# A transformer layer in float32: the first norm's gain and bias applied behind the transposes and later in token layout, with the residual loaded in place

## The chip, the cores and the metric

One core of a Trainium2 chip runs the whole kernel. The metric is the device time of one execution in microseconds (us), the median over several runs.

## The reference

One layer on x of 1024 tokens by 1024 features, all in float32 (S = D = 1024, F = 2816):

```
h    = x @ w_in                                  # attention heads and a gated spatial group
mix  = concat(diff_attention(h), spatial_gate(h)) @ w_out
x    = layer_norm(ALPHA * x + mix, ln1_g, ln1_b) # the first norm
g    = causal_conv3(x @ w_gate)                  # along the tokens
up   = x @ w_up
f    = (silu(g) * up) @ w_down
x    = layer_norm(ALPHA * x + f, ln2_g, ln2_b)   # the second norm
```

where layer_norm(y, g, b) = (y - mean) * rstd * g + b, with mean and rstd of each token.

## The kernel before

Every float32 product runs as three matmuls: each operand is split into a high part (written by ACT in `split`, L216) and a low part (the rest, by DVE, L217), and L221 to L223 add hi·hi, hi·lo and lo·hi into one PSUM tile. Four engines work beside TensorE (PE): VectorE (DVE), ScalarE (ACT), GpSimd (POOL), and SyncE (SP), whose queue issues most DMAs. Each engine runs its instructions in order; a scheduler that builds the program chooses the order and which buffer a new tile takes, and puts a wait on the last user of that buffer.

The work comes in five stages (times in the profiled execution).

- **Projections and attention**, 0 to 365 us.
- **Output projection**, 365 to 434 us: `mix` for each token tile t of 128 tokens. `fill_x` adds ALPHA·x (loaded by `x_load` into a tile of its own, `xn`) to the product and takes the norm's statistics; `lnorm` then computes the norm. It takes the statistics together (DVE `bn_aggr`), adds EPS, raises to the power -1/2 on POOL (L889), then for each half of 512 columns: (x - mean) * g on DVE (L891), times rstd on ACT (L893) or on DVE (L896), plus b on POOL (L894).
- **Gate stage**, 434 to about 866 us: x @ w_gate and x @ w_up in 22 units u (even: gate, odd: up). A unit is a 2 by 2 block product by Strassen's scheme: seven products P1 to P7 instead of eight, each 12 matmuls of 128x512. Their x operands are A11, A12, A22 and the sums S1 to S4 (QA), their weight operands B11, B21, B22 and the differences T1 to T4 (QB). Tokens 0 to 511 give A11 and A12, tokens 512 to 1023 A21 and A22; each needs x with features on the partitions, so `x1_transp(t)` transposes tile t on PE (L930) and ACT copies it from PSUM (`fA`, L938), and `x1_sums` forms S2 on DVE (L948), S4 on POOL (L950); A22 is added straight from PSUM into S1 (DVE L935) and S3 is formed on POOL (L936). Four products of the first two units run before the sums are needed; `fill_in` puts the transposes of the last two token tiles behind the products i = 0 and i = 1 of `seq`, the sums behind i = 2 and 3.
- **Down stage**, about 866 to 1087 us: the same scheme with w_down (operands `yo` and `do`), in the order of DORDER, P4 and P3 last. `d_out` adds a product's PSUM into x; `finish(t)` is the second norm and the store of tile t. Tiles 4 to 7 are finished behind P4, tiles 0 to 3 behind the last matmuls of P3.
- **Tail**, to 1096 us: the last tile's norm and its store.

In the gate stage a weight quarter is loaded into one of 8 raw buffers (`tslot`, tile `wq`), DVE forms the differences in place (L972), and ACT and DVE write the split operand (`wT`, `wB`) into one of 16 buffers (`kslot`), some seven products ahead of its use. P4, P6 and P7 of a unit add up in one PSUM tile, and ACT copies it out after each (L1009 to L1020), so the next of them waits for that copy:

```
        elif name == "P6":
            A.copy(d1[:, LEFT], a)
        elif name == "P7":
            A.copy(d1[:, RIGHT], a)
```

Of the kernel before, what the change touches and what calls it, by code (L numbers as in the profile page):

```python
# [138 lines left out]
def hybrid_layer_kernel(  # L139
# [735 lines left out]
    def load_row(pool, ap_, name):  # L875
        t = pool.tile([P, D], F32, name=name)
        GP.dma_start(t, bc_row(ap_, D))
        return t

    g1 = load_row(op, ln1_g, "g1")  # L880
    b1 = load_row(op, ln1_b, "b1")
    x1T = {}
# [309 lines left out]
    fill_in = [  # L1192
        lambda: x1_transp(6), lambda: x1_transp(7), lambda: (x1_sums("S1"), prepare(1)),
        lambda: (x1_sums("S2"), prepare(4), x1_sums("S3"), prepare(5), x1_sums("S4")),
    ]
# [65 lines left out]
    for n, name in enumerate(DORDER):  # L1261
# [79 lines left out]
```

## Time and profile before

| | |
|---|---|
| median of 3 runs | 1097.71 us (1096.16 to 1100.11) |
| the profiled execution | 1097.62 us, span 1095.8 us |
| PE, DVE, ACT, POOL busy | 1060.0, 785.4, 485.0, 189.3 us |
| mean granted clock of PE | 0.988 of full speed |

The span is what the trace covers; the rest of an execution's time, 1.8 us, lies around it. A wait is the idle time of an engine ahead of an instruction, put down to the event that released it.

### The profile page before, as it was taken

What the parts mean: (1) busy time and instruction counts of PE and PEld (TensorE: products, weight loads), DVE (VectorE), ACT (ScalarE), POOL (GpSimd) and SP (SyncE); (2) the same over time, 40 slices, a digit from 0 to 9 for tenths busy, and PEclk for the clock granted to TensorE, in tenths of its full rate; (3) what the DMA queues carried; (4) which work ended last, traced back from release to release, by engine and by line L of the source; (5) the groups of instructions that cost most, each with busy time, mean ns of one, the idle gap of its engine ahead of it and who ended that gap; (6) DMA issues with size and microseconds to landing.
All of it is one profiled execution on the core that took longest, in us unless ns stands there. A gap on an engine that the chain in (4) does not pass through costs nothing.

```text
span 1095.8 us, 14041 instructions
## 1 busy us (share of the span) xinstructions
PE 1060.0 (97%) x4974; PEld 874.2 (80%) x4974; DVE 785.4 (72%) x1308; ACT 485.0 (44%) x901; POOL 189.3 (17%) x213
## 2 busy tenths in 40 slices
PE   8999999987999999899999999999999999999996
PEld 6888888876787888678888888888888878888874
DVE  5327246669999648997687677768777589954786
ACT  5511113456777335555344434434544254444441
POOL 2014132228643036400000000000000000000045
PEclk9999999999999999899999999999999999999997
DMA  8400214442200511033332232233235983432322
GB/s 260 150 10 10 96 57 126 107 116 59 58 11 20 181 50 49 11 115 113 118 124 69 106 125 86 104 110 126 67 109 175 315 287 94 135 106 87 106 86 96
DMA packets 57574, 115.92 MB, mean 106 GB/s; under 512 B 7392, under 2 KB 7920, under 8 KB 57504
## 3 DMA queue, kind: packets, MB, share of 16 engines
q1 hardware_dynamic: 56464, 111.70, 31.1%
q0 software_dynamic: 1040, 3.32, 1.1%
q8 instruction: 39, 0.64, 0.2%
q14 instruction: 31, 0.25, 0.1%
HBM read 82.23 MB, written 24.38 MB: 97 GB/s over the span
## 4 chain that ended last, share of the span: by engine, by line
PE 84%; DVE 8%; issue 3%; POOL 3%; DMA 1%; SPq 1%; ACT 0%; DVEq 0%; POOLq 0%; ACTq 0%
PE ps L222 26%; PE ps L221 26%; PE ps L223 26%; PE ps L622 2%; PE ps L608 1%; PE ps L545 1%; PE ps L546 1%; DVE x L891 1%; POOL kl L475 1%; PE ps L357 1%; DVE p L591 1%; DVE mx L558 1%; DMA dq<-w_down 1%; DVE wT L217 0%; PE ps L930 0%
## 5 line engine op out<-in xcount | busy, mean ns | idle before, releaser
L222 PE MATMUL ps<-do,yo 128*128 128x512 f32 x308 | 122.2, 397 | 2.7 <-DVE do L217 2.7
L221 PE MATMUL ps<-do,yo 128*128 128x512 f32 x308 | 120.7, 393 | 2.3 <-ACT do L216 2.3
L223 PE MATMUL ps<-do,yo 128*128 128x512 f32 x308 | 121.6, 395 | 0.0
L217 DVE TENSOR_TENSOR wT<-wq,wT 128x512 fp32r<-128x512 f32 x88 | 63.1, 719 | 34.2 <-ACT wT L216 34.1
L1268 POOL DMA_DIRECT2D g<-ln_g x1 | 0.6, 578 | 477.3 <-DVE do L217 477.3
L216 ACT ACTIVATE wT<-wq 128x512 fp32r<-128x512 f32 x88 | 55.3, 632 | 50.6 <-PE ps L223 43.5
L217 DVE TENSOR_TENSOR yo<-ya,yo 128x512 fp32r<-128x512 f32 x77 | 55.0, 715 | 23.9 <-ACT yo L216 23.8
L222 PEld LDWEIGHTS ps<-do,yo 128*128 128x128 f32 x308 | 58.9, 191 | 16.6 <-DVE do L217 4.2
L221 PEld LDWEIGHTS ps<-do,yo 128*128 128x128 f32 x308 | 58.5, 190 | 14.8 <-ACT do L216 2.8
L216 ACT ACTIVATE yo<-ya 128x512 fp32r<-128x512 f32 x77 | 48.3, 627 | 48.1 <-PE ps L223 46.9
L223 PEld LDWEIGHTS ps<-do,yo 128*128 128x128 f32 x308 | 59.1, 192 | 12.4
L217 DVE TENSOR_TENSOR wB<-wq,wB 128x512 fp32r<-128x512 f32 x66 | 45.8, 697 | 26.8 <-ACT wB L216 20.4
L217 DVE TENSOR_TENSOR do<-dq,do 128x512 fp32r<-128x512 f32 x66 | 47.4, 718 | 23.3 <-ACT do L216 23.3
L216 ACT ACTIVATE wB<-wq 128x512 fp32r<-128x512 f32 x66 | 41.1, 630 | 48.4 <-PE ps L223 33.5
L972 DVE TENSOR_TENSOR wq<-wq,wq 128x512 f32<-128x512 f32 x88 | 60.7, 690 | 2.6
L216 ACT ACTIVATE do<-dq 128x512 fp32r<-128x512 f32 x66 | 41.2, 624 | 48.1 <-DVE yo L217 17.3
L1038 DVE SCALAR_TENSOR_TENSOR c<-g,cw,c 128x1023 f32<-128x1023 f32 (+1 forms) x44 | 56.3, 1279 | 6.5 <-ACT c L1036 6.4
L570 ACT ACTIVATE p<-ps,mx 128x512 f32<-128x512 f32 (+7 forms) x64 | 47.1, 742 | 9.0 <-DVE mx L558 5.9
L221 PE MATMUL ps<-xh,qw 128*128 128x512 f32 x128 | 49.9, 390 | 0.0
L222 PE MATMUL ps<-xl,qw 128*128 128x512 f32 x128 | 49.8, 389 | 0.0
L223 PE MATMUL ps<-xh,qw 128*128 128x512 f32 x128 | 49.8, 389 | 0.0
L221 PE MATMUL ps<-zw,xh 128*128 128x512 f32 x128 | 49.8, 389 | 0.0
(244 smaller groups left out, 2935.8 us busy)
## 6 DMA issues: line engine op xcount, KB each, us to landing
ya<-yd SPq DMA_DIRECT2D x77, 256.0 KB, 2.9
wq<-w_gate SPq DMA_DIRECT2D x44, 256.0 KB, 2.8
wq<-w_up SPq DMA_DIRECT2D x44, 256.0 KB, 2.8
yd<-u SPq DMA_DIRECT2D x22, 512.0 KB, 3.1
dq<-w_down SPq DMA_DIRECT2D x44, 256.0 KB, 4.6
zraw<-w_vz SPq DMA_DIRECT2D x23, 256.0 KB, 3.0
yd<-c SPq DMA_DIRECT2D x11, 512.0 KB, 2.6
qraw<-w_qk SPq DMA_DIRECT2D x8, 512.0 KB, 4.2
```

Of the source, the lines that this page charges most:

```text
L216: A.activation(hi, src, AF.Copy)
L217: (lo_eng or V).tensor_tensor(lo, src, hi.bitcast(F32), op=ALU.subtract)
L221: PE.matmul(po, lhsT=lh, rhs=rh, start=start, stop=False, skip_group_check=onto)
L222: PE.matmul(po, lhsT=lh, rhs=rl, start=False, stop=False, skip_group_check=onto)
L223: PE.matmul(po, lhsT=ll, rhs=rh, start=False, stop=stop, skip_group_check=onto)
L357: PE.matmul(pt[:, c, :], lhsT=vg[t // 2][:, t % 2, g * P : (g + 1) * P], rhs=wsr[:, g, :], start=True, stop=True)
L475: eng.tensor_tensor(o, r[rows], hi, op=ALU.subtract)
L545: PE.matmul(o[:, 0:ww], lhsT=qs[:, qc], rhs=kh[:, kc], start=True, stop=False)
L570: A.activation(p[:, 0:L].rearrange("p (b n) -> p b n", b=nb), sc, AF.Exp, bias=st_mx[n][:, j : j + 1], accum_out=sm[:, j : j + 1],)
L622: PE.matmul(st_o[h, i][:, j * DV : (j + 1) * DV], lhsT=st_at[h, i][kt // 4][:, kt % 4, j], rhs=vr[kt // 2][:, kt % 2, h * DV : (h + 1) * D ...
L972: sub = lambda o, a, b: V.tensor_tensor(q[o], q[a], q[b], op=ALU.subtract)
L1038: V.scalar_tensor_tensor(t[:, n:S], g[:, 0 : S - n], cw[:, f, 2 - n : 3 - n], t[:, n:S], op0=ALU.mult, op1=ALU.add)
```

## The change

The first norm's gain and bias are no longer applied where the norm is computed. `standard(t)` writes (x - mean) * rstd alone: DVE takes the statistics together and forms two small terms, POOL computes rstd and -mean * rstd, and one ACT instruction scales and shifts the whole tile. The gain and bias are applied in two other places:

- behind the transposes, where a feature is a partition: ACT's eviction of each transposed block takes them as a scale and a bias per partition (`gb1`). Transposes come in pairs of token tiles; the last pair stands behind product i = 2. A22 is now written to SBUF too, so the splits and sums read SBUF, and S3 and S4 are formed on DVE.
- in token layout, for the residual of the second norm: `gain(t, c)` on POOL, a multiplication and an addition per half tile, in the gate stage, with g and b of one half broadcast into a `kslot` buffer `gb`.

The right half of x for the residual is loaded straight into x1; the weight quarters of units 0 and 1 are all loaded at t = 3; `finish(4)` to `finish(7)` move from behind P4 to P3's m = 1 to 4, and weights of the last two products are prepared up to 3 steps earlier.

```diff
+    def standard(t):
+        mv = op.tile([P, 32], F32, tag="mv", name=nm("mv"), bufs=3)[:, 0:3]
+        rs = op.tile([P, 32], F32, tag="rs", name=nm("rs"), bufs=3)[:, 0:2]
+        V.bn_aggr(mv[:, 0:2], stats[t])
+        V.tensor_scalar(rs[:, 0:1], mv[:, 1:2], EPS, None, op0=ALU.add)
+        V.tensor_scalar(mv[:, 2:3], mv[:, 0:1], -1.0, None, op0=ALU.mult)
+        GP.tensor_tensor(rs[:, 0:1], rs[:, 0:1], mhalf[:, 0:1], op=ALU.pow)
+        GP.tensor_tensor(rs[:, 1:2], rs[:, 0:1], mv[:, 2:3], op=ALU.mult)
+        A.activation(x1[t], x1[t], AF.Identity, scale=rs[:, 0:1], bias=rs[:, 1:2])
...
         for eg, name in enumerate(names):
-            pt = ps1().rearrange("p (e q) -> p e q", e=4)
-            for e in range(4):
-                PE.transpose(pt[:, e, :], x1[t][:, (eg * 4 + e) * P : (eg * 4 + e + 1) * P], ident)
             for n in range(2):
-                src = pt[:, 2 * n : 2 * n + 2, :]
-                if name == "A22":
-                    f = xf["A21"][n][:, :, tk]
-                    V.tensor_tensor(xf["S1"][n][:, :, tk], f, src, op=ALU.add)
-                    GP.tensor_tensor(f, xf["A11"][n][:, :, tk], f, op=ALU.subtract)
-                else:
-                    A.copy(xf[name][n][:, :, tk], src)
+                pt = ps1().rearrange("p (e q) -> p e q", e=2)
+                f = xf["S1" if name == "A22" else name][n][:, :, tk]
+                for e in range(2):
+                    k = eg * 4 + n * 2 + e
+                    for i in range(2):
+                        PE.transpose(pt[:, e, i * P : (i + 1) * P], x1[t + i][:, k * P : (k + 1) * P], ident)
+                    A.activation(f[:, e], pt[:, e], AF.Identity, scale=gb1[:, 0, k : k + 1], bias=gb1[:, 1, k : k + 1])
                 if name != "A21":
                     hi, lo = xo[name][n]
-                    split(hi[:, :, tk], lo[:, :, tk], src)
+                    split(hi[:, :, tk], lo[:, :, tk], f)
+                if name == "A22":
+                    V.tensor_tensor(f, xf["A21"][n][:, :, tk], f, op=ALU.add)
...
-            if name == "S2":
-                V.tensor_tensor(xf[o][n], xf["S1"][n], xf["A11"][n], op=ALU.subtract)
-            elif name == "S4":
-                GP.tensor_tensor(xf[o][n], xf["A12"][n], xf["S1"][n], op=ALU.subtract)
+            if a:
+                V.tensor_tensor(xf[o][n], xf[a][n], xf[b][n], op=ALU.subtract)
...
     for t in range(NT):
-        x_load(t, 1)
+        nc.sync.dma_start(x1[t][:, RIGHT], x[t * P : (t + 1) * P, RIGHT])
+    for t in range(NT):
...
         fill_x(t, pt, 1)
-        lnorm(op, x1[t], stats[t], x1[t], g1, b1, None, t < NT - 1)
-        if 2 <= t < 6:
-            x1_transp(t - 2)
+        standard(t)
+        if t in (3, 5):
+            x1_transp(t - 3)
+        if t == 3:
+            for u in range(2):
+                w_load(u, ("B11", "B21"))
+            for u in range(2):
+                w_load(u, ("B12", "B22"))
...
+    def gain(t, c):
+        h = RIGHT if c else LEFT
+        if t == 0:
+            gb[c] = kslot([P, 2, 512], "gb", F32)
+            GP.dma_start(gb[c][:, 0], bc_row(ln1_g[h], 512))
+            GP.dma_start(gb[c][:, 1], bc_row(ln1_b[h], 512))
+        r = x1[t][:, h]
+        GP.tensor_tensor(r, r, gb[c][:, 0], op=ALU.mult)
+        GP.tensor_tensor(r, r, gb[c][:, 1], op=ALU.add)
+
+    gains = {(u + 3, "P4"): (u % NT, u // NT) for u in range(2 * NT)}
...
         elif name == "P4":
             start(hi[:, LEFT])
             norm_stats(4 + j, 0)
-            finish(4 + j)
...
-            d_prepare(n * NM + m + DAHEAD)
+            d_prepare(n * NM + m + DAHEAD + (max(0, min(3, m - 3)) if name == "P4" else 3 if name == "P3" else 0))
+            if name == "P3" and m:
+                finish(3 + m)
```

How this changes the order of the instructions is shown at three places. The number after an underscore tells tiles of one name apart.

**POOL at the start of the gate stage.** Before: the S3 differences (L936), the two S4 differences (L950) and then, 480 us later, the second norm's g and b.

```order
185 L936 TENSOR_TENSOR fA_4136<-fA_3822,fA_4136 128x2x128 [waits DVE_49,Activation_49]
186 L950 TENSOR_TENSOR fA_3827<-fA_3827,fA_4141 128x1024 [waits DVE_49]
187 L950 TENSOR_TENSOR fA_3828<-fA_3828,fA_4142 128x1024 [waits DVE_49]
188 L1268 DMA g_8610<-ln_g 128x1024 [waits DVE_49,Pool_49]
189 L1268 DMA b_8612<-ln_b 128x1024 [waits DVE_49]
190 L889 TENSOR_TENSOR rs_8824<-rs_8824,mhalf 128x1 [waits DVE_49]
```

Now: the last of `standard`'s small terms, then the DMAs of `gb`, then the 16 multiplications and additions of all 8 token tiles' left halves, of which the first five are shown. The first DMA's waits are the only ones on PE or DVE; the PE one is the end of P6 of unit 3.

```order
174 L903 TENSOR_TENSOR rs_4089<-rs_4089,mv_4088 128x1 [waits DVE_49,Pool_49]
175 L1210 DMA gb_4776<-ln_g 128x512 [waits DVE_49,PE_49]
176 L1211 DMA gb_4776<-ln_b 128x512
177 L1213 TENSOR_TENSOR x_3546<-x_3546,gb_4776 128x512 [waits DMASW1_49]
178 L1213 TENSOR_TENSOR x_3539<-x_3539,gb_4776 128x512
179 L1214 TENSOR_TENSOR x_3546<-x_3546,gb_4776 128x512 [waits DMASW2_49,Pool_49]
180 L1214 TENSOR_TENSOR x_3539<-x_3539,gb_4776 128x512 [waits Pool_49]
181 L1213 TENSOR_TENSOR x_3525<-x_3525,gb_4776 128x512
```

So the 16 instructions, which the code places one pair per unit, stand in one row behind one DMA; the same two DMAs and 16 instructions follow for the right halves, behind P6 of unit 11.

**ACT around the weights of unit 5.** The split of B21 of unit 5, before (`wB_4901`), with its neighbours: it waits for its DMA and for PE.

```order
411 L216 ACTIVATE wB_4869<-wq_4861 128x512 [waits DMAHW4_49]
412 L1015 COPY u_4638<-ps_824_4624 128x512 [waits PE_49]
413 L216 ACTIVATE wT_4885<-wq_4725 128x512
414 L216 ACTIVATE wB_4901<-wq_4863 128x512 [waits DMAHW5_49,PE_49]
415 L216 ACTIVATE wT_4921<-wq_4723 128x512 [waits DVE_49,PE_49]
416 L216 ACTIVATE wT_4939<-wq_4861 128x512 [waits DVE_49,PE_49]
417 L216 ACTIVATE wB_4956<-wq_4867 128x512 [waits DMAHW7_49,PE_49]
418 L1013 COPY g_4778<-ps_842_4764 128x512 [waits PE_49]
```

Now the same split (`wB_4849`) has taken the buffer of the first `gb`: it waits for both `gb` DMAs and for POOL, whose awaited instruction is the last of the 16. Behind it stand three more splits and the copy of P6 of unit 4 (`g_4721`), in order.

```order
402 L217 ACTIVATE wB_4817<-wq_4809 128x512 [waits DMAHW4_49]
403 L217 ACTIVATE wT_4833<-wq_4668 128x512 [waits PE_49]
404 L217 ACTIVATE wB_4849<-wq_4811 128x512 [waits DMASW2_49,DMAHW5_49,DMASW1_49,Pool_49]
405 L217 ACTIVATE wT_4869<-wq_4666 128x512 [waits DVE_49,PE_49]
406 L217 ACTIVATE wT_4887<-wq_4809 128x512 [waits DVE_49,PE_49]
407 L217 ACTIVATE wB_4904<-wq_4815 128x512 [waits DMAHW7_49,PE_49]
408 L1021 COPY g_4721<-ps_834_4707 128x512 [waits PE_49]
```

The order of these splits and copies has stayed; what a split waits for has changed.

**DVE in the first products of unit 1.** Before: the splits of S2 to S4, with S2 formed here (L948) and S3 and S4 on POOL.

```order
546 L1011 TENSOR_TENSOR u_4283<-u_4283,ps_777_4299 128x512 [waits PE_49]
547 L948 TENSOR_TENSOR fA_4141<-fA_4141,fA_3821 128x1024 [waits DVE_49]
548 L948 TENSOR_TENSOR fA_4142<-fA_4142,fA_3822 128x1024 [waits DVE_49]
549 L217 TENSOR_TENSOR wT_4328<-wq_4047,wT_4328 128x512 [waits Activation_49]
550 L217 TENSOR_TENSOR S2l_4315<-fA_4141,S2h_4313 128x1024 [waits Activation_49]
551 L217 TENSOR_TENSOR S2l_4316<-fA_4142,S2h_4314 128x1024 [waits Activation_49]
552 L217 TENSOR_TENSOR S3l_4333<-fA_4135,S3h_4331 128x1024 [waits Pool_49]
553 L217 TENSOR_TENSOR S3l_4334<-fA_4136,S3h_4332 128x1024 [waits Activation_49]
554 L217 TENSOR_TENSOR wT_4339<-wq_4225,wT_4339 128x512 [waits Activation_49]
555 L217 TENSOR_TENSOR S4l_4344<-fA_3827,S4h_4342 128x1024 [waits Activation_49]
556 L972 TENSOR_TENSOR wq_4323<-wq_4325,wq_4323 128x512 [waits DMAHW3_49]
557 L217 TENSOR_TENSOR S4l_4345<-fA_3828,S4h_4343 128x1024 [waits DVE_49,Activation_49]
```

Now six differences (L958), those of S2 (`fA_4102`, `fA_4103`), S3 and S4, all run on DVE; the weight split of T3 (`wT_4282`) stands behind them, and the two of S4 behind it.

```order
530 L218 TENSOR_TENSOR S1l_4252<-fA_4103,S1h_4250 128x1024 [waits Activation_49]
531 L958 TENSOR_TENSOR fA_4102<-fA_4102,fA_3848 128x1024 [waits DVE_49]
532 L958 TENSOR_TENSOR fA_4103<-fA_4103,fA_3849 128x1024 [waits DVE_49]
533 L958 TENSOR_TENSOR fA_4096<-fA_3848,fA_4096 128x1024
534 L218 TENSOR_TENSOR S2l_4264<-fA_4102,S2h_4262 128x1024 [waits Activation_49]
535 L218 TENSOR_TENSOR S2l_4265<-fA_4103,S2h_4263 128x1024 [waits Activation_49]
536 L218 TENSOR_TENSOR S3l_4274<-fA_4096,S3h_4272 128x1024 [waits Activation_49]
537 L958 TENSOR_TENSOR fA_4097<-fA_3849,fA_4097 128x1024
538 L958 TENSOR_TENSOR fA_3854<-fA_3854,fA_4102 128x1024
539 L958 TENSOR_TENSOR fA_3855<-fA_3855,fA_4103 128x1024
540 L218 TENSOR_TENSOR S3l_4275<-fA_4097,S3h_4273 128x1024 [waits Activation_49]
541 L218 TENSOR_TENSOR wT_4282<-wq_3900,wT_4282 128x512 [waits PE_49,Activation_49]
```

Each instruction of DVE behind the differences has moved back by up to four of them.

## Rows read from the trace of the kernel before

**Rows 1.** The page, part 1: busy time of each engine.

```profile
PE 1060.0 (97%) x4974; PEld 874.2 (80%) x4974; DVE 785.4 (72%) x1308; ACT 485.0 (44%) x901; POOL 189.3 (17%) x213
```

**Rows 2.** Windows: stretch, length, busy PE, PEld, DVE, ACT, POOL, clock, DMA share, GB/s.

```profile
424.00:434.00 10.00, 10.00 (x46) 8.29 (x45) 7.09 (x17) 4.17 (x9) 5.92 (x5) 1.00 0.17 53
...
455.00:465.00 10.00, 7.39 (x22) 5.38 (x23) 10.00 (x7) 3.76 (x6) 4.41 (x2) 0.66 0.00 0
...
500.00:860.00 360.00, 360.00 (x1590) 298.08 (x1589) 269.75 (x378) 162.09 (x244) 0.00 (x0) 1.00 0.33 113
860.00:885.00 25.00, 22.67 (x94) 18.13 (x94) 11.41 (x19) 6.58 (x12) 0.00 (x0) 0.94 0.96 346
...
1048.00:1096.00 48.00, 36.66 (x147) 28.69 (x145) 37.42 (x58) 13.87 (x22) 27.86 (x22) 0.87 0.25 93
```

**Rows 3.** Timeline of PE, 442 to 470 us: start, duration, engine, line, operation, releaser.

```profile
457.23 0.80 PE L223 MATMUL ps<-S1h,wT 128*128 128x512 f32 x1 [2.32 <-DVE wT L217]
...
469.89 0.50 PE L221 MATMUL ps<-S2h,wT 128*128 128x512 f32 x1 [2.08 <-ACT wT L216]
```

**Rows 4.** Timeline of DVE, 434 to 480 us.

```profile
454.33 2.85 DVE L217 TENSOR_TENSOR wT<-wq,wT 128x512 fp32r<-128x512 f32 x1
457.10 4.52 DVE L217 TENSOR_TENSOR S2l<-fA,S2h 128x1024 fp32r<-128x1024 f32 x2
461.54 2.35 DVE L217 TENSOR_TENSOR S3l<-fA,S3h 128x1024 fp32r<-128x1024 f32 x2
```

**Rows 5.** Timeline of POOL, same stretch.

```profile
453.35 6.06 POOL L950 TENSOR_TENSOR fA<-fA,fA 128x1024 f32<-128x1024 f32 x2 [4.96 <-DVE fA L948]
```

**Rows 6.** Timeline of all engines, 424 to 434 us: the norm of one token tile.

```profile
428.96 0.69 DVE L904 SCALAR_TENSOR_TENSOR x<-xn,ps 128x512 f32<-128x512 f32 x1 [1.54 <-PE ps L223]
...
431.31 0.99 POOL L889 TENSOR_TENSOR rs<-rs,mhalf 128x1 f32<-128x1 f32 x1 [1.50 <-DVE rs L888]
...
432.33 1.34 ACT L893 ACTIVATE x<-x,rs 128x512 f32<-128x512 f32 x2 [5.06 <-POOL rs L889]
...
433.13 1.29 POOL L894 TENSOR_TENSOR x<-x,b 128x512 f32<-128x512 f32 x1 [0.83 <-ACT x L893]
```

**Rows 7.** Timeline of ACT, 366 to 368 us.

```profile
367.55 0.47 ACT L668 ACTIVATE oT<-ps,sg 128x256 fp32r<-128x256 f32 x1 [2.22 <-PE ps L662]
```

**Rows 8.** Timeline of ACT, 514 to 550 us.

```profile
516.48 0.59 ACT L1013 COPY u<-ps 128x512 f32<-128x512 f32 x1 [1.12 <-PE ps L223]
...
524.64 0.63 ACT L216 ACTIVATE wB<-wq 128x512 fp32r<-128x512 f32 x1 [1.60 <-PE ps L223]
...
535.52 0.59 ACT L1013 COPY g<-ps 128x512 f32<-128x512 f32 x1 [2.09 <-PE ps L223]
...
538.24 0.59 ACT L1009 COPY u<-ps 128x512 f32<-128x512 f32 x1 [1.60 <-PE ps L223]
```

**Rows 9.** DMA issues: queue, count, size of each, median time to landing.

```profile
glg<-gln_g POOLq DMA_DIRECT2D x1, 256.0 KB, 4.9
```

**Rows 10.** Timeline of POOL, 1050 to 1096 us.

```profile
1053.09 1.01 POOL L889 TENSOR_TENSOR rs<-rs,mhalf 128x1 f32<-128x1 f32 x1 [113.67 <-DVE rs L888]
...
1061.25 4.68 POOL L894 TENSOR_TENSOR x<-x,b 128x512 f32<-128x512 f32 x3
...
1067.72 3.44 POOL L894 TENSOR_TENSOR x<-x,b 128x512 f32<-128x512 f32 x2 [0.83 <-ACT x L893]
...
1085.57 0.99 POOL L889 TENSOR_TENSOR rs<-rs,mhalf 128x1 f32<-128x1 f32 x1
...
1089.84 0.99 POOL L889 TENSOR_TENSOR rs<-rs,mhalf 128x1 f32<-128x1 f32 x1
```

**Rows 11.** Timeline of DVE, same stretch.

```profile
1061.39 1.70 DVE L217 TENSOR_TENSOR do<-dq,do 128x512 fp32r<-128x512 f32 x1
...
1067.07 0.68 DVE L217 TENSOR_TENSOR do<-dq,do 128x512 fp32r<-128x512 f32 x1
```

**Rows 12.** The page, part 5: a group: busy us, mean ns, idle before, releaser.

```profile
L222 PE MATMUL ps<-do,yo 128*128 128x512 f32 x308 | 122.2, 397 | 2.7 <-DVE do L217 2.7
```

More of the change, by code (lines that the diff above doesn't have):

```diff
@@ L163, in hybrid_layer_kernel @@
     sin_t: bass.AP,
+    ln1_c: bass.AP,
     out: bass.AP,
@@ L229, in hybrid_layer_kernel @@
     m_r = const.tile([P, 64], BF16, name="m_r")
-    lam4 = const.tile([P, 4, 64], F32, name="lam4")
+    const.tile([P, 42], F32, name="pad")
     nlam = const.tile([P, 1], F32, name="nlam")
@@ L234, in hybrid_layer_kernel @@
     cb = const.tile([P, NF], F32, name="cb")
+    gb1 = const.tile([P, 2, NK], F32, name="gb1")
     zp = tc.alloc_tile_pool(name="zp", bufs=1)
@@ L285, in hybrid_layer_kernel @@
     glb = zq.tile([P, ATT], F32, name="glb")
+    lam4 = zp.tile([P, 4, 64], F32, name="lam4")
     wsr = zp.tile([P, H, P], F32, name="wsr")
@@ L295, in hybrid_layer_kernel @@
     GP.dma_start(cb, conv_b)
+    GP.dma_start(gb1, ln1_c)
     GP.affine_select(
@@ L873, in hybrid_layer_kernel @@
     op = tc.alloc_tile_pool(name="op", bufs=1, reuse_waits="tile")
[L875 to L882, printed above, removed]
     def lnorm(pool, r, st, o, g, b, after=None, spread=False):
-        mv = pool.tile([P, 32], F32, tag="mv", name=nm("mv"), bufs=3)[:, 0:2]
+        mv = pool.tile([P, 2], F32, tag="mv", name=nm("mv"), bufs=3)
         V.bn_aggr(mv, st)
-        rs = pool.tile([P, 32], F32, tag="rs", name=nm("rs"), bufs=3)[:, 0:1]
+        rs = pool.tile([P, 1], F32, tag="rs", name=nm("rs"), bufs=3)
         V.tensor_scalar(rs, mv[:, 1:2], EPS, None, op0=ALU.add)
@@ L903, in fill_x @@
         cols = slice(c * 512, (c + 1) * 512)
-        V.scalar_tensor_tensor(x1[t][:, cols], acc[t, c], ALPHA, pt, op0=ALU.mult, op1=ALU.add)
+        src = x1[t][:, cols] if c else acc[t, c]
+        V.scalar_tensor_tensor(x1[t][:, cols], src, ALPHA, pt, op0=ALU.mult, op1=ALU.add)
         V.bn_stats(stats[t][:, c, :], x1[t][:, cols])
@@ L919, in x1_transp @@
     def x1_transp(t):
-        tk = slice((t % 4) * P, (t % 4 + 1) * P)
+        tk = slice((t % 4) * P, (t % 4 + 2) * P)
         names = ("A11", "A12") if t < 4 else ("A21", "A22")
@@ L1087, in hybrid_layer_kernel @@
         fill_x(t, pt, 1)
-        lnorm(op, x1[t], stats[t], x1[t], g1, b1, None, t < NT - 1)
-        if 2 <= t < 6:
-            x1_transp(t - 2)
+        standard(t)
[6 more added lines that the diff above has]
+                w_load(u, ("B12", "B22"))
         if t == 5:
             for u in range(2):
-                w_load(u, ("B11", "B21"))
                 w_prep(u, "B11")
@@ L1096, in hybrid_layer_kernel @@
     x1_transp(4)
-    x1_transp(5)
-    fp = None
     NU = NF
@@ L1191, in hybrid_layer_kernel @@
     dram = tc.alloc_tile_pool(name="dram", bufs=1, space=bass.MemoryType.DRAM)
[L1192 to L1195, printed above, removed]
+    gb = {}
+    def gain(t, c):
[8 more added lines that the diff above has]
+    gains = {(u + 3, "P4"): (u % NT, u // NT) for u in range(2 * NT)}
+    fill_in = {
+        2: lambda: x1_transp(6),
+        3: lambda: (x1_sums("S1"), prepare(1)),
+        4: lambda: (x1_sums("S2"), prepare(4), x1_sums("S3"), prepare(5), x1_sums("S4")),
+    }
     for i, (u, name) in enumerate(seq):
         prepare(max(0, i + AHEAD - 4))
+        if i == 4:
+            fill_in[i]()
         product(u, name)
+        if i < 4 and i in fill_in:
+            fill_in[i]()
         outputs(u, name)
-        if i < len(fill_in):
-            fill_in[i]()
+        if (u, name) in gains:
+            gain(*gains[u, name])
         if (u, name) == (NU - 1, "P2"):
@@ L1332 @@
         "sin_t": lay(np.concatenate([-sin, sin] * 2, axis=0)),
+        "ln1_c": lay(np.stack([v["ln1_g"][0].reshape(NK, P).T, v["ln1_b"][0].reshape(NK, P).T], axis=1)),
     }
```

5 lines of the change are left out of this document (4 added, 1 removed).

## The prediction

> **What bounds the kernel now.** I read the busy times first. PE works for 1060.0 us of a span of 1095.8 [rows 1], so no other engine's total can be the bound; an edit matters only where it makes PE wait or frees it from a wait. The windows say where PE waits now. In the output projection it doesn't: 10.00 us busy of 10 between 424 and 434. In the gate stage it doesn't either, 360.00 of 360 between 500 and 860, although DVE, ACT and the weight loads all work there. It waits in three places: at the start of the gate stage, at the change to the down stage (2.33 us idle between 860 and 885, not touched by the change), and at the end [rows 2]. After each the clock falls to its half level (1.2 of 2.4 GHz) for a while. A product of 12 matmuls takes 538.24 - 535.52 = 2.72 us at the full level [rows 8], 0.227 each, so the 94 matmuls of 860 to 885 should take 21.3 us; they took 22.67, and 1.4 us went to the clock. The same sum gives 2.4 us for the 22 matmuls of 455 to 465 and 3.3 us for the 147 behind 1048.
>
> At the gate start the long waits are for DVE's weight split at 457.23 (2.32 us) and for the weight split that follows DVE's chain at 469.89 (2.08 us) [rows 3]. At the end PE waits 2.7 us in all for DVE's `do` splits [rows 12].
>
> **Term 1, the norm and the first sums of the gate stage: +3.5 us (+1.2 to +6), and +1.3 us (0 to 3) of clock.** Gone are DVE's L891, ACT's two scalings and POOL's two additions per tile: 1.34 us from ACT at 432.33 and 1.29 us for each addition [rows 6]. What comes is one ACT instruction of 128x1024 (two such halves take 1.34) and a multiplication on POOL of the size of the power beside it, at most 0.99 us. But PE had no wait in this stage, so the removed work hid behind its 24 matmuls per tile. What is new on PE's path is the eviction: ACT, in order, has to run `standard` of the tile that was just filled (fill at 428.96, power at 431.31, ACT at 432.33) before its evictions of the pair's blocks, and the second half of each PSUM tile waits for the eviction of the first. Walked on these rows, PE loses 1.07 us at t = 3, 0.15 at t = 5 and 1.2 behind the loop.
>
> Then the last pair of tiles is transposed behind product i = 2 (near 446.6 us) instead of tile 6 behind i = 0 and tile 7 behind i = 1. Eight evictions with a scale and a bias come on ACT; the nearest is a 128x256 with one scale from memory, 0.47 us [rows 7], and I take 0.42 behind each other. A22 is then there near 450.8 and S1's high half near 454.1. From there DVE runs two S1 splits, six differences, two splits each of S2 and S3, that is 12 of 128x1024, a weight split between them, T3's split, two S4 splits, and two 128x512 ahead of T2's split on ACT. A 128x1024 costs 2.35 / 2 = 1.13 to 1.2 us when POOL is idle [rows 4], a 128x512 0.60 to 0.68 [rows 11]: 14.2 us to the end of S3 and 4.1 more. That is 472.7, ACT's split 0.63 [rows 8], and PE goes on at 473.4 instead of 469.89: +3.5, in which the 1.2 behind the loop is already contained, as is what PE lost at t = 3, since all later work waits for the same chain. Were DVE never without work from the first eviction on (21.8 us from 448.6), it would be +1.2; +6 if each wait of PE moves on separately. PE's idle time there grows by as much, so I add half of the 2.4 us that the clock cost there.
>
> One rule speaks of this place. POOL's S4 differences (6.06 us for two [rows 5]) ran beside a DVE weight split that took 2.85 us and two S2 splits that took 4.52 [rows 4]; alone these take 0.68 and 2.35, so POOL cost DVE 4.4 us. Moving S3 and S4 to DVE adds 4 x 1.13 = 4.5 us to it. The two cancel, which is why the lateness of the transposes decides this term. The Trainium skill, "SBUF — State Buffer", section "SBUF: two separate sides", says that DVE and GpSimd share a port pair as an exclusive lock, held for a whole instruction, against which a DVE operation with two SBUF inputs blocks. The trace agrees: `do` took 1.70 us beside POOL's additions [rows 10, 11] and 0.68 alone.
>
> **Term 2, the gain and bias in the gate stage: +18.8 us (0 to +36), and +3.4 us (0 to 6) of clock.** The code puts two POOL instructions into each unit, but POOL's order has one wait only: the first DMA of `gb` waits for P6 of unit 3, which ends at 516.48 [rows 8]. A 256 KB broadcast lands in 4.9 us [rows 9]. So from about 521.5 POOL runs 16 instructions in one go; each costs 1.29 us alone [rows 6] and 4.68 / 3 = 1.56 beside DVE's two-input work [rows 10], 20.6 to 25 us in all, to between 542 and 546.5. I take 543, since DVE soon stops too. ACT's split of B21 of unit 5, which ran at 524.64 [rows 8], now waits for the last of the 16, as it takes `gb`'s buffer. ACT runs in order, so behind this wait are three splits and the copy of P6 of unit 4, which ran at 535.52, and P7 of unit 4 adds to the PSUM tile that this copy reads. Four splits and the copy make 2.9 us at 0.5 to 0.63 each: P7 starts at 545.9 instead of 538.24, +7.6. Weights are then no longer ahead, so the copy of P7, behind T2's split on ACT and its two DVE differences, holds up P4 by another 1.75: 9.4 us. The second burst has the same queue behind it (P6 of unit 11, B21 of unit 13), so 2 x 9.4 = 18.8. The bounds: nothing, if the lead of the weights covers it all; 18 us a burst if POOL and DVE alternate throughout. What hides the same work elsewhere is just this lead, some seven products or 16 to 19 us; a burst of 21.5 that begins 5 us behind P6 is longer than what is left of it. Behind each wait the clock falls; I take 1.7 us, between the 1.4 behind the 2.33-us wait and the 2.4 above.
>
> **Term 3, the end: -2.3 us (-6 to +1).** `finish(4)` to `finish(7)` stand behind the splits of P3's first steps now, so the `do` splits no longer queue behind POOL-slowed work: PE's 2.7 us of waits and the 3.3 us of clock can go. But POOL then binds. Its four first norms took 1053.09 to 1067.72 + 3.44 = 1071.16, 4.5 each; the last ones follow each other at 1089.84 - 1085.57 = 4.3 [rows 10]. The first power now comes about 3 us later, near 1056.1, behind four starts, four statistics and the splits. Then 1056.1 + 4 x 4.5 + 3 x 4.3 = 1087.0 for the last power, and with half a microsecond for DVE's alternation 1087.5, against 1089.84.
>
> **At nothing.** The residual loads, the earlier weight loads and the other addresses: their issue is on SP and their data land under PE's busy stretch of the output projection; without that cover a load of 256 KB costs about 5 us [rows 9].
>
> **The sum.** The profiled execution took 1097.62 us (span 1095.8 and 1.8 around it), 0.1 below the median, so it stands for it: 1097.62 + 3.5 + 1.3 + 18.8 + 3.4 - 2.3 = 1122.3; I say 1122.
>
> **The rivals.**
> - *The bursts stay under the lead of the weights.* For: PE has no wait there now, and the splits run seven products ahead. Against: the copy of P6 stands behind the blocked split in ACT's order. It holds if the burst ends by about 535, that is if a POOL instruction takes 0.85 us; the nearest row says 1.29. Then 1097.6 + 4.8 - 2.3 = 1100 (1096 to 1105).
> - *Faster: the end decides.* If the bursts are hidden so, the DVE chain is bound by its work alone (+1.2) and POOL's chain follows PE's end by as little as before, the 6 us of waits and clock at the end come back whole: 1097.6 + 1.2 - 6 = 1093. It needs POOL's power 3 us earlier than I walk it.
> - *The bursts alternate.* If every POOL instruction is followed by one of DVE, a burst takes 16 x (1.29 + 0.60) = 30 us and ends at 551.5; P7 starts 16 us late, with P4 18 us a burst: 1122.3 + 2 x 8.4 = 1139. Against: DVE itself soon waits for the blocked ACT split. That is the lock of the page named above, taken for the whole burst; rows 10 and 11 show it for a few instructions only.
>
> **Chances.** The forecast, 1112 to 1131: 0.65. Hidden bursts, or bursts that cost a third, 1096 to 1111: 0.17. Faster by the end: 0.06. Alternating bursts, 1132 and above: 0.12. A change under 0.3% (3.3 us) can't be told from none here: of the second case I give 0.05 to a result within it. So faster 0.07, same 0.06, slower 0.87; the range runs from 1102, within the second case, to 1133.
>
> **What will show it.** PE idle near 538 to 546 us, ended by an ACT copy, and again some eight units later; ACT idle from about 525, ended by a POOL addition; 16 POOL instructions back to back. At the gate start a PE wait that ends near 473 in before's time. At the end no PE wait for `do`, and a last power of POOL near 1087 counted without the earlier loss. Wrong it would be, above all, if POOL's instructions turn out spread over the units, or if PE's wait ends with the weights' DVE work instead of the copy.

## The result and the profile after

The changed kernel takes 1125.66 us (median of 4 runs, 1123.71 to 1127.5) beside 1098.1 for the kernel before (also 4 runs, one more than in the table of before): a ratio of 1.025, 95% interval 1.0228 to 1.0271. The profiled execution took 1125.54 us, with a span of 1123.8. It is slower, as forecast (1122, range 1102 to 1133).

The windows of the trace after, in the columns of [rows 2]:

```profile
455.00:465.00 10.00, 7.58 (x20) 5.73 (x21) 10.00 (x12) 5.55 (x6) 0.00 (x0) 0.66 0.08 26
465.00:475.00 10.00, 7.73 (x26) 5.51 (x25) 9.49 (x10) 4.47 (x6) 0.00 (x0) 0.80 0.09 26
475.00:500.00 25.00, 23.80 (x101) 19.07 (x101) 22.48 (x34) 15.50 (x23) 0.00 (x0) 0.94 0.29 95
...
520.00:560.00 40.00, 31.75 (x131) 25.74 (x130) 24.39 (x30) 10.04 (x16) 23.32 (x18) 0.87 0.23 73
560.00:720.00 160.00, 152.10 (x667) 125.42 (x666) 114.71 (x157) 66.12 (x100) 23.29 (x18) 0.98 0.29 97
```

PE now waits in the middle of the gate stage too, where it waited for nothing before: 8.25 us between 520 and 560 and 7.9 between 560 and 720. Its granted clock is below full in the windows that hold these waits, and at the gate start in three windows (0.66, 0.80 and 0.94), where before only the first of them was. The view of PE's waits by releaser shows what ended them (total, times, longest):

```profile
engine line waited for: us in total, times, longest us
PE ps L222 <- ACT g L1021: 16.2, 2, 8.3
...
PE ps L222 <- ACT wT L217: 3.4, 2, 2.2
```

The 16.2 us in two waits for an ACT copy (`g`, L1021, the copy of P6) are the largest. The `do` waits on DVE [rows 12] are gone. The long waits of the gate start, in the timeline of PE, answer to [rows 3]:

```profile
456.37 0.72 PE L222 MATMUL ps<-S1h,wT 128*128 128x512 f32 x2 [2.69 <-ACT S1h L217]
...
471.09 0.80 PE L222 MATMUL ps<-S3h,wT 128*128 128x512 f32 x1 [2.15 <-ACT wT L217]
...
478.27 0.51 PE L222 MATMUL ps<-S2h,wT 128*128 128x512 f32 x1 [1.21 <-ACT wT L217]
```

**Where the time went.** The span grew by 28.0 us. The same events of both traces, compared, give the parts:

| place | event, before and after | added so far | part |
|---|---|---|---|
| ahead of the second half of the output projection | `fill_x` of the first half's last tile, 387.30 and 388.72 | 1.4 | 1.4 |
| its second half | `fill_x` of the last tile, 434.40 and 437.85 | 3.45 | 2.0 |
| gate start | copy of P6 of unit 3, 516.48 and 524.83 | 8.35 | 4.9 |
| first burst | P7 of unit 4 starts, 538.24 and 554.81 | 16.57 | 8.2 |
| its clock, second burst | PE's wait for `do` in the down stage ends, 880.67 and 910.46 | 29.8 | 13.2 |
| end | last power on POOL, 1089.84 and 1118.34 | 28.5 | -1.3 |

The span grew by half a microsecond less than this, nearly all of it in the last power itself: 0.99 us before [rows 10], 0.55 now. The 1.4 us of the first row are not the change's: in the traces of the experiments this event lies between 386.88 and 389.00, and at 389.00 and 388.86 in e4 and e9, whose code up to there is that of the kernel before.

**The burst itself.** POOL's timeline in the changed kernel, first and last rows of the first burst:

```profile
525.10 0.65 POOL L1210 DMA_DIRECT2D gb<-ln_g  x1 [84.37 <-PE ps L224]
...
529.95 2.54 POOL L1213 TENSOR_TENSOR x<-x,gb 128x512 f32<-128x512 f32 x2 [3.65 <-DMA gb<-ln_g]
...
549.58 2.48 POOL L1214 TENSOR_TENSOR x<-x,gb 128x512 f32<-128x512 f32 x2
```

ACT's timeline beside it:

```profile
532.99 0.63 ACT L217 ACTIVATE wT<-wq 128x512 fp32r<-128x512 f32 x1 [1.60 <-PE ps L224]
552.10 0.63 ACT L217 ACTIVATE wB<-wq 128x512 fp32r<-128x512 f32 x1 [18.47 <-POOL x L1214]
552.63 1.13 ACT L217 ACTIVATE wT<-wq 128x512 fp32r<-128x512 f32 x2
...
554.19 0.56 ACT L1021 COPY g<-ps 128x512 f32<-128x512 f32 x1
```

And PE's:

```profile
554.81 0.79 PE L222 MATMUL ps<-S3h,wT 128*128 128x512 f32 x1 [8.25 <-ACT g L1021]
...
559.93 0.40 PE L222 MATMUL ps<-A12h,wB 128*128 128x512 f32 x1
```

POOL runs 16 instructions from 529.95 to 552.06. ACT's split of B21 waits 18.47 us for the last of them; three splits and the copy of P6 follow within 2.6 us, and PE, idle for 8.25 us, starts P7 the moment the copy's result is there. P7's 12 matmuls then take 559.93 - 554.81 = 5.1 us instead of 2.7, since they run at the half clock (1.2 GHz): 0.43 us from one to the next, against 0.23.

### The profile page after: what moved, and what is told of

Read it like the earlier page. It is cut to its first block, busy times and chain, and to the rows that moved or that the text cites. A ratio compares the mean times of both kernels' runs of the same rounds, so it can differ in the third digit from the quotient of the medians.

```text
span 1123.8 us, 13996 instructions
## 1 busy us (share of the span) xinstructions
PE 1069.3 (95%) x4974; PEld 879.9 (78%) x4974; DVE 779.2 (69%) x1286; ACT 491.6 (44%) x891; POOL 200.9 (18%) x232
## 3 DMA queue, kind: packets, MB, share of 16 engines
q0 software_dynamic: 1104, 3.33, 1.2%
## 4 chain that ended last, share of the span: by engine, by line
PE 78%; POOL 8%; DVE 4%; issue 3%; ACT 3%; DMA 2%; SPq 1%; POOLq 0%; DVEq 0%; ACTq 0%
PE ps L222 24%; PE ps L224 24%; PE ps L223 24%; PE ps L626 2%; POOL x L1214 2%; POOL x L1213 2%; POOL x L889 2%; PE ps L612 1%; PE ps L549 1%; PE ps L550 1%; POOL kl L479 1%; DMA gb<-ln_g 1%; PE ps L361 1%; DVE mx L562 1%; DVE p L595 1%
## 5 line engine op out<-in xcount | busy, mean ns | idle before, releaser
L980 DVE TENSOR_TENSOR wq<-wq,wq 128x512 f32<-128x512 f32 x88 | 65.0, 740 | 2.6
L222 PE MATMUL ps<-S3h,wT 128*128 128x512 f32 x88 | 37.7, 428 | 18.3 <-ACT g L1021 16.2
```

The source lines that it names most:

```text
L222: PE.matmul(po, lhsT=lh, rhs=rh, start=start, stop=False, skip_group_check=onto)
L980: sub = lambda o, a, b: V.tensor_tensor(q[o], q[a], q[b], op=ALU.subtract)
```

## The experiments

Each ratio is to runs of the kernel before on the same chip. To compare kernels of different chips, a ratio is told in us on the 1098.1 us of the kernel before: the changed kernel's 1.025 is +27.5 us.

**e1: no gain and bias in token layout.**

```diff
-    gains = {(u + 3, "P4"): (u % NT, u // NT) for u in range(2 * NT)}
+    gains = {}
```

> The changed kernel without the 32 multiplications and additions of gain and bias in token layout and without the buffer gb (the second norm's residual then lacks them; all else is as changed). Theory: the two POOL bursts cost 21.8 us through ACT's wait for gb's buffer (two PE waits of 8.25 and 7.90 us and the half clock behind them), so 1125.7 - 21.8 = 1104 us, and no PE wait between 480 and 880 us. Rival: the loss is in the gate stage's start and the late chain alone, and the bursts only showed what was lost anyway: above 1115.

Measured: 1103.03 us, ratio 1.0026 (1.0012 to 1.0039), or +2.9 us. PE is busy without a gap between 500 and 860:

```profile
500.00:860.00 360.00, 360.00 (x1590) 298.10 (x1589) 268.52 (x379) 159.45 (x240) 0.00 (x0) 1.00 0.32 113
```

By the medians the token-layout work costs 24.6 of the 27.5 us (from the ends of the two intervals 20.7 to 28.5), and the rest of the change 2.9 (1.3 to 4.3). In the traces, from the copy of P6 of unit 3 to the end of PE's wait for `do` in the down stage, PE takes 364.2 us before, 385.6 in the changed kernel and 364.0 in e1: 21.6 us lie in this stretch. The profiled execution of e1 took 1099.39 us, 3.6 less than its median; where that can come from stands under term 1 below.

**e2: a fresh buffer for each half tile.**

```diff
-        if t == 0:
-            gb[c] = kslot([P, 2, 512], "gb", F32)
-            GP.dma_start(gb[c][:, 0], bc_row(ln1_g[h], 512))
-            GP.dma_start(gb[c][:, 1], bc_row(ln1_b[h], 512))
+        gb[c] = kslot([P, 2, 512], "gb", F32)
+        GP.dma_start(gb[c][:, 0], bc_row(ln1_g[h], 512))
+        GP.dma_start(gb[c][:, 1], bc_row(ln1_b[h], 512))
```

> The changed kernel with gb loaded anew for each of the 16 half tiles, so that each buffer is held for one multiplication and one addition only; the same 32 POOL instructions, 14 more pairs of DMAs. Theory (ACT waits for a buffer that POOL holds too long): the two PE waits vanish though POOL does the same work, 1104 to 1106 us. Rival (POOL's work slows DVE through the shared port, wherever it stands): the loss stays, spread over the units, 1115 to 1126 us.

Measured: 1122.56 us, ratio 1.022 (1.0203 to 1.0237), or +24.2. The theory's time (1104 to 1106) is missed and the rival's met, but the waits end with ACT's copy behind a split that waited for POOL's buffer, not with DVE's work as the rival had it. PE now waits in each of 16 units, 0.3 to 3.0 us, 18 us in all. ACT's and PE's timelines around the first:

```profile
526.44 0.63 ACT L217 ACTIVATE wT<-wq 128x512 fp32r<-128x512 f32 x1
531.09 0.63 ACT L217 ACTIVATE wB<-wq 128x512 fp32r<-128x512 f32 x1 [4.01 <-POOL x L1213]
531.62 0.57 ACT L1023 COPY u<-ps 128x512 f32<-128x512 f32 x1
```

```profile
532.24 0.50 PE L222 MATMUL ps<-A22h,wT 128*128 128x512 f32 x1 [0.88 <-ACT u L1023]
```

POOL holds the buffer for its DMAs' landing and two instructions, some 7.6 us, and ACT's next split but one takes it: ACT stands for 4.01 us and the copy of P7 (L1023) behind it is late for P4. So even a short hold hurts, which the theory had not seen. The lead of the weights, seven products, doesn't count here; what counts is the copy, which has less than a product's time.

**e3: half the burst.**

```diff
-        if (u, name) in gains:
+        if (u, name) in gains and gains[u, name][0] < NT // 2:
```

> The changed kernel with gain and bias in token layout for the token tiles 0 to 3 only (tiles 4 to 7 go into the second norm's residual without them): two bursts of 8 POOL instructions instead of 16. Theory: a burst of 8 ends about 10 us earlier, near 541 us, and ACT's four or five splits and its copy are done by 545, before P7 of unit 4 is due at 546.5: the lead of the weights hides it, both waits vanish, 1104 us. Rival (the cost goes with the number of POOL instructions): half of it stays, 1115 us.

Measured: 1107.27 us, ratio 1.0066 (1.0045 to 1.0087), or +7.2, 4.3 above e1, clear of both intervals. P7's waits vanish, as the theory said, but its time of 1104 is missed, for P4 of the same unit waits 1.99 and 1.56 us. ACT's timeline:

```profile
540.79 0.63 ACT L217 ACTIVATE wT<-wq 128x512 fp32r<-128x512 f32 x1 [9.59 <-POOL x L1214]
...
551.63 0.63 ACT L217 ACTIVATE wT<-wq 128x512 fp32r<-128x512 f32 x1 [5.96 <-DVE wq L980]
...
553.16 0.57 ACT L1023 COPY g<-ps 128x512 f32<-128x512 f32 x1
```

ACT was free at 541, yet at 551.63 its split of T2 still waits for DVE's differences (L980), which had waited for ACT, and the copy of P7 (L1023, 553.16) comes behind. That is the second wait of the prediction's term 2. The cost is not in proportion to POOL's work: half of it costs 4.3 us, all of it 24.6.

**e5: the same bursts without a buffer.**

```diff
+        pin = dst_w[u][1][:, 0:1]
+        for t in range(NT):
+            GP.tensor_tensor(x1[t][:, h][:, 0:1], x1[t][:, h][:, 0:1], pin, op=ALU.add)
+        for t in range(NT):
+            r = x1[t][:, h]
+            GP.tensor_tensor(r, r, r, op=ALU.add)
+            GP.tensor_tensor(r, r, r, op=ALU.subtract)
```

(in place of `gain`'s body; called behind P6 of units 3 and 11)

> The changed kernel with two bursts of 16 POOL instructions of 128x512 behind P6 of units 3 and 11, as in the changed kernel, but without gb and its DMAs: each instruction adds or subtracts the half tile to or from itself (so the residual is zero and the output is not the reference's), and eight additions of one column hold the burst behind P6. No weight buffer waits for POOL. Theory (the loss is ACT's wait for gb's buffer, with the PSUM copies queued behind it): no PE wait between 500 and 880 us, 1103 to 1105 us. Rival (POOL's 32 instructions slow DVE through the port that they share, and that is the loss): 1115 us and above.

Measured: 1104.04 us, ratio 1.005 (1.0034 to 1.0066), or +5.5, 2.6 above e1 with intervals that overlap. POOL's and DVE's timelines in the middle of the burst:

```profile
529.26 2.93 POOL L1212 TENSOR_TENSOR x<-x 128x512 f32<-128x512 f32 x2
```

```profile
538.46 1.52 DVE L1057 TENSOR_TENSOR u<-c 128x512 f32<-128x512 f32 x1
...
541.35 0.67 DVE L1026 TENSOR_TENSOR u<-u,ps 128x512 f32<-128x512 f32 x1
```

A DVE operation with SBUF inputs takes 1.52 us beside POOL instead of 0.68 and alternates with it for all of the burst; one with a PSUM input (L1026) keeps its 0.67. Even so PE loses only 0.74 us per burst. From the copy of P6 of unit 3 to the end of the wait in the down stage PE takes 366.5 us, against 364.0 in e1 and 385.6 in the changed kernel. This separates the two causes: POOL's work beside DVE costs some 2.5 us in this stretch, the wait for its buffer is the loss.

**e8: a buffer outside the ring.**

```diff
-            gb[c] = kslot([P, 2, 512], "gb", F32)
+            gb[c] = fp.tile([P, 2, P], F32, tag="gb", name=nm("gb"), bufs=1)
```

(eight column blocks of 128 instead of two halves)

> The changed kernel with gain and bias in token layout done in eight column blocks of 128 with a buffer of 1 KB per partition outside the ring of the weights: 128 POOL instructions of 128x128, some 59 us of POOL work instead of 41 to 46, none of which a weight split waits for. Theory (buffer wait): 1103 to 1106 us. Rival (POOL's work beside DVE): above 1115.

Measured: 1104.03 us, ratio 1.0059 (1.0037 to 1.0081), or +6.5, as the theory said: 21 us less than the changed kernel, with 128 POOL instructions instead of 32. What it loses against e1 is not where the bursts were: the stretch named above takes 364.0 us in both traces. It is at the gate start, where POOL now begins early, beside DVE's chain (see e10): from the last `fill_x` to the copy of P6 of unit 3 it takes 89.9 us, 85.3 in e1.

**e6: transposes one product earlier.** On e1:

```diff
-        2: lambda: x1_transp(6),
+        1: lambda: x1_transp(6),
```

> The kernel e1 (no gain and bias in token layout) with the transposes of the last two token tiles behind product i = 1 instead of i = 2, one product of 2.72 us earlier. Theory (the lateness of the transposes sets when PE resumes): the first wait for S1, 2.7 us, goes, and the chain behind it starts up to 2.7 us earlier: 1100.5 us against e1's 1103. Rival (DVE's work alone sets it, or ACT's evictions do): 1103, with the same wait moved to the weights of T2 and T3.

Measured: 1098.66 us, ratio 1.0005 (0.9991 to 1.002), or +0.5: 2.4 us less than e1, against 2.5 expected. The two intervals touch (e1's begins at 1.0012); the traces bear the gain out. PE's timeline, and the first window of the gate start:

```profile
455.44 0.50 PE L223 MATMUL ps<-S1l,wT 128*128 128x512 f32 x1 [0.75 <-DVE S1l L218]
...
473.52 0.50 PE L222 MATMUL ps<-S2h,wT 128*128 128x512 f32 x1 [1.75 <-ACT wT L217]
```

```profile
455.00:465.00 10.00, 7.88 (x32) 5.88 (x33) 10.00 (x11) 3.18 (x3) 0.00 (x0) 1.00 0.00 0
```

The wait for S1's high half (2.69 us) is gone, and none of the gate start's waits that are left is above 1.8 us. The granted clock stays full there (1.00, against 0.66 in e1 and in the kernel before). From the last `fill_x` to the copy of P6 of unit 3 it takes 82.0 us, waits and clock together: 3.2 less than e1 (85.3), and as much as the kernel before (82.1).

**e7: S3 and S4 on POOL again.** On e1:

```diff
-                V.tensor_tensor(xf[o][n], xf[a][n], xf[b][n], op=ALU.subtract)
+                (V if name == "S2" else GP).tensor_tensor(xf[o][n], xf[a][n], xf[b][n], op=ALU.subtract)
```

> The kernel e1 with the four differences of S3 and S4 on POOL instead of DVE (4 x 1.13 us off DVE). Theory (what POOL takes over it costs DVE again as blocked time, 4.4 us in the kernel before): within 1 us of e1, 1103. Rival (DVE's chain becomes shorter by its own work): 1099. Rival (a POOL difference of 128x1024 takes 3 us, and S3 and S4 come later than on DVE): 1106.

Measured: 1108.47 us, ratio 1.0084 (1.0065 to 1.0102), or +9.2, 6.3 above e1. POOL's, DVE's and PE's timelines:

```profile
459.37 3.21 POOL L958 TENSOR_TENSOR fA<-fA,fA 128x1024 f32<-128x1024 f32 x1 [1.29 <-DVE fA L948]
```

```profile
460.29 2.85 DVE L218 TENSOR_TENSOR wT<-wq,wT 128x512 fp32r<-128x512 f32 x1
...
469.80 4.49 DVE L218 TENSOR_TENSOR S2l<-fA,S2h 128x1024 fp32r<-128x1024 f32 x2
```

```profile
473.21 0.79 PE L223 MATMUL ps<-S2l,wT 128*128 128x512 f32 x1 [5.16 <-DVE S2l L218]
```

The theory fails; the last rival holds, and more: a difference of 128x1024 takes POOL 3.21 us against DVE's 1.13, and while POOL's differences run, a weight split of 0.68 us ahead of S1's second takes 2.85 and S2's splits 4.49 instead of 2.35, so PE waits 5.16 us for S2. The gate start alone, between the events named under e6, takes 91.6 us, 6.3 more than e1's.

**e4: the moved finish alone, on the kernel before.**

```diff
             norm_stats(4 + j, 0)
-            finish(4 + j)
...
-            d_prepare(n * NM + m + DAHEAD)
+            d_prepare(n * NM + m + DAHEAD + (max(0, min(3, m - 3)) if name == "P4" else 3 if name == "P3" else 0))
+            if name == "P3" and m:
+                finish(3 + m)
```

> The kernel before with only the end of the change: the finish of tiles 4 to 7 moved from behind P4 to P3's steps 1 to 4, and the weights of the last products prepared up to 3 steps earlier. Theory: PE's 2.7 us of waits for do and the 3.3 us of half clock go, but POOL's chain of eight norms binds, so 2.0 to 2.5 us are won: 1095.8 us. Rival (PE's waits were the end's price in full): 5 to 6 us, 1092.5. Rival (POOL starts later and its chain is the end): no gain, 1098.

Measured: 1096.82 us, ratio 0.9982 (0.9967 to 0.9996): 2.0 us won (0.4 to 3.6). PE's waits for DVE's `do` splits are gone; POOL's first and last power:

```profile
1058.00 1.01 POOL L889 TENSOR_TENSOR rs<-rs,mhalf 128x1 f32<-128x1 f32 x1 [116.68 <-DVE rs L888]
...
1090.47 0.55 POOL L889 TENSOR_TENSOR rs<-rs,mhalf 128x1 f32<-128x1 f32 x1
```

The eight norms take 32.5 us back to back, 36.8 before with gaps [rows 10]: POOL's chain is the end.

**e9: e4 and S4 on DVE, on the kernel before.**

```diff
-                GP.tensor_tensor(xf[o][n], xf["A12"][n], xf["S1"][n], op=ALU.subtract)
+                V.tensor_tensor(xf[o][n], xf["A12"][n], xf["S1"][n], op=ALU.subtract)
```

> The kernel before with the moved finish of e4 and, besides, the two S4 differences on DVE instead of POOL (L950). Theory (DVE lost 4.4 us blocked by POOL there and gets 2.3 us of work instead, as e7 showed the other way round): the waits of 2.3 us at 457 and 2.1 us at 470 shrink by some 2 us together and the half clock behind them by 1: 1094 us, against 1096.8 of e4. Rival (S4 then comes later in DVE's order and the weights of T2 with it): as e4, 1096.8, or worse.

Measured: 1093.69 us, ratio 0.9956 (0.994 to 0.9972), or -4.8 (-6.6 to -3.1): faster than both kernels, and 2.8 faster than e4. The intervals of e4 and e9 just touch; in the traces the gate start takes 82.1 us in e4 and 79.5 here, waits and clock together, which is nearly all of the 2.8. DVE's and PE's timelines:

```profile
455.89 0.68 DVE L217 TENSOR_TENSOR wT<-wq,wT 128x512 fp32r<-128x512 f32 x1
...
461.63 2.35 DVE L950 TENSOR_TENSOR fA<-fA,fA 128x1024 f32<-128x1024 f32 x2
```

```profile
471.41 0.50 PE L221 MATMUL ps<-S2h,wT 128*128 128x512 f32 x1 [0.91 <-ACT wT L216]
```

The weight split that took 2.85 us [rows 4] takes 0.68, PE's wait of 2.32 us for it is gone and that for T2 falls from 2.08 to 0.91. A new wait of 1.40 us, for a DVE addition (L1016), stands before it at 467.45.

**e10 and e11: both losses mended.** e10 is e8 with e6's transposes; e11 adds, ahead of each block's DMA of g,

```diff
+            GP.tensor_copy(gb[c][:, 0, 0:1], dst_w[u][0][:, 0:1])
```

> The changed kernel with both of its losses mended: the gain and bias buffer of e8 outside the ring of the weights, and the transposes of the last pair behind i = 1 as in e6. The output is the reference's. Theory (the two losses add up): 1104.0 - 4.4 = 1099.6 us, that is the time of the kernel before within 0.3%. Rival (POOL's early column blocks run beside DVE's chain at the gate start and take the gain of the earlier transposes): 1103.

> The kernel e10 with one added copy of a column per column block on POOL, which reads what unit u + 3 has written, so that a block's POOL work can't begin before that unit. Theory (in e10, whose POOL work began at 443 us, the port cost DVE's chain at the gate start what the earlier transposes had won): POOL is idle from 440 to 500 us, S3's splits take 1.2 us again instead of 1.5, and the time is that of e6 with up to 1 us for the work later: 1098.7 to 1100 us. Rival (the loss of e10 is spread over the units, as 128 instructions on POOL): 1104.

e10: 1104.32 us, ratio 1.0063 (1.0047 to 1.0079), or +6.9: as the rival said. With a buffer of its own nothing holds POOL back, and it begins at 443 us, beside DVE's chain, as in e8. POOL's and DVE's timelines:

```profile
461.10 6.68 POOL L1214 TENSOR_TENSOR x<-x,gb 128x128 f32<-128x128 f32 x5 [2.11 <-DMA gb<-ln_g]
```

```profile
470.18 1.47 DVE L218 TENSOR_TENSOR S3l<-fA,S3h 128x1024 fp32r<-128x1024 f32 x1
```

e11: 1098.42 us, ratio 0.9996 (0.9985 to 1.0008): the time of the kernel before. Its windows show POOL idle at the gate start, and 133 us of POOL work in a stage in which PE does not wait at all:

```profile
440.00:480.00 40.00, 33.00 (x138) 24.06 (x138) 34.94 (x44) 26.73 (x45) 0.33 (x1) 0.96 0.17 54
...
500.00:860.00 360.00, 360.00 (x1590) 298.10 (x1589) 285.23 (x378) 160.21 (x242) 132.78 (x151) 1.00 0.35 115
```

## Why the prediction was right

**The step that carried it** was the wait of B21's split for `gb`'s buffer, with the copy of P6 behind it. P7's wait was worked out as 7.6 us and is 8.25 and 7.90; the burst's end as 543 in before's time and it was 552.1 - 8.35 = 543.7. e5 and e11 show that POOL's work alone costs some 2.5 us or none, e1 and e8 that the loss goes with the buffer. Term 2, 22.2 us with its clock, measured 21.4 in the trace and 24.6 by e1. That the sum came out within 1 us is in part luck, since its parts were traded: P7's two waits were 0.9 us longer than forecast and the half clock behind them took 2.4 us each, which was counted as 1.7; against that P4 did not wait its 1.75 us behind either. P7 took those 2.4 us longer and so gave ACT and DVE time. Behind the second burst ACT's copy of P7 and P4's first matmul stand so:

```profile
724.79 0.58 ACT L1023 COPY g<-ps 128x512 f32<-128x512 f32 x1
...
725.99 0.39 PE L222 MATMUL ps<-A22h,wT 128*128 128x512 f32 x1
```

The copy ends at 725.4; at the full clock P4 would have been due at 725.99 - 2.4 = 723.6, an estimate, and would have waited the 1.8 us. In e3, where P7 did not wait, P4's wait is there.

**Term 1 was too small**: 4.8 us forecast, 2.0 + 4.9 = 6.9 in this trace, but 2.0 + 3.2 = 5.2 in e1's, whose code is the same up to the burst. By the medians it is e1's 2.9 and the 2.0 that e4 won, 4.9, with some 1.5 us of uncertainty on each. So the miss lies between nothing and 2 us. The mechanism held: evictions held up the transposes for 0.56, 0.68 and 0.62 us (forecast 1.07, 0.15 and 1.2), the chain from the late transposes to T2's split of unit 1 set PE's resumption, and in e6, with them one product earlier, the gate start takes 3.2 us less, waits and clock together. But PE went on at 478.27, or 476.9 without the 1.4 of the stages ahead, not at 473.4; in e1 it did at 475.17. What differs is the clock. In the changed kernel:

```profile
471.09 0.80 PE L222 MATMUL ps<-S3h,wT 128*128 128x512 f32 x1 [2.15 <-ACT wT L217]
471.69 0.63 PE L223 MATMUL ps<-S3l,wT 128*128 128x512 f32 x1
```

In e1:

```profile
469.56 0.50 PE L222 MATMUL ps<-S3h,wT 128*128 128x512 f32 x1 [2.15 <-ACT wT L217]
469.90 0.40 PE L223 MATMUL ps<-S3l,wT 128*128 128x512 f32 x1
```

The same wait of 2.15 us is followed by the half clock in one execution and by the full one in the other. e2's gate start is as long as e1's (85.2 us), e3's and e5's as the changed kernel's (87.0), with the same code. So the clock, put at 1.3 us more than before, is a term that changes from one trace to the next by some 1.7 us, and the length of the waits does not tell which it will be. Nor had it fallen behind each long wait before: behind the 2.08 us at 469.89 it stayed full (2.4 GHz; 1.00 from 465 to 475). And 0.8 us of the output projection's 2.0 is in no wait; the transposes there run in twos between matmuls, but no run measured that by itself. Two slips in the working, 454.1 + 14.2 + 4.1 = 472.4 and not 472.7, and half of 2.4 counted as 1.3, make 0.4 us and decide nothing.

**"The two cancel" failed.** The prediction held that moving S3 and S4 to DVE changes nothing, since 4.4 us of blocked time go and 4.5 of work come. By e7 POOL's way costs 6.3 us more in the changed kernel, and by e9 against e4 2.8 us more (S4 alone) in the one before. Sums of DVE's time said "equal". What differs, by the rows of e7 and e9, is what the time delays: a blocked weight split holds PE at once, DVE's own differences stand ahead of splits that PE needs later, and POOL takes nearly three times as long to deliver the sum. No run took these three apart. So this part of the change was a gain hidden in a loss. The lock that the Trainium skill describes ("SBUF — State Buffer", "SBUF: two separate sides") is borne out by e5's rows: 1.52 against 0.68 us, and 0.67 with a PSUM input.

**Term 3** was forecast at -2.3 us and is -1.3 to -1.8 in the trace, -2.0 by e4. Here too the clock has its share: behind the wait at the change to the down stage it fell in the changed kernel (a wait of 1.93 us; 0.72 from 910 to 916), and stayed full in e1 (2.13 us; 1.00 from 885 to 895), whose last power came 1.6 us sooner behind that wait. These 1.6 and the 1.7 of term 1 would make most of the 3.6 us by which e1's profiled execution lies under its median; the other executions have no trace, so this is not shown. First and last power:

```profile
1085.88 1.00 POOL L884 TENSOR_TENSOR rs<-rs,mhalf 128x1 f32<-128x1 f32 x1 [116.67 <-DVE rs L883]
...
1118.34 0.55 POOL L884 TENSOR_TENSOR rs<-rs,mhalf 128x1 f32<-128x1 f32 x1
```

The eight norms follow each other for 32.5 us, POOL's chain as forecast; the last power came 1118.34 - 29.8 = 1088.5 in before's time, against 1087.5.

**The rivals.** Hidden bursts: refuted, though e8 and e11 show that they are hidden once no weight waits for them. Faster by the end: refuted, POOL's chain binds. Alternating bursts: in the changed kernel DVE stopped soon, as argued, and the burst took 22.1 us, not 30; e5, where it did alternate, shows that alternation by itself would have cost little. Left open are the 0.8 us above, and why the same wait is followed by the half clock in some executions only.

## What to carry to other kernels

A buffer taken from a ring for a slow, low-priority job is a promise that the ring's next user can wait. Look up which instruction takes that buffer next, and then what stands behind it on that engine: here a weight split with seven products of lead, and behind it a PSUM copy with less than one. And where a tile is placed per unit in the code, check in the order of the queue that something really holds it there: the same gain and bias cost 25 us in bursts with the ring's buffer, 7 us beside a busy chain (e10 against e11), and nothing where they were pinned to a quiet stretch.

## What the runs showed of the hardware

A POOL operation that reads one SBUF tile twice (e5) blocks DVE as one with two tiles does: 1.52 us, against 1.53 to 1.77 in the changed kernel's burst. The price for DVE goes with the length of the POOL instruction: a 128x512 DVE operation with two SBUF inputs takes 0.68 us alone, 0.94 beside 128x128 POOL work (e10), 1.5 to 1.8 beside 128x512, and 2.85 beside 128x1024 (e7). The half clock behind a wait of 8.25 us cost 2.4 us, that behind one of 2.33 us 1.4; but it does not go with the wait alone. In the changed kernel 12 matmuls behind the 2.15 us at 471.09 ran at it, 12 x (0.43 - 0.23) = 2.4 us by estimate; in e1 none did behind a wait just as long. In e2 a wait of 2.40 us was followed by it, and one of 3.00 us was not:

```profile
594.81 0.50 PE L222 MATMUL ps<-A22h,wT 128*128 128x512 f32 x1 [3.00 <-ACT g L1023]
...
781.15 0.79 PE L222 MATMUL ps<-A22h,wT 128*128 128x512 f32 x1 [2.40 <-ACT u L1023]
782.17 0.63 PE L224 MATMUL ps<-A22h,wT 128*128 128x512 f32 x1
```
